# A hybrid mLSTM/HGRN2 layer on one core: first HGRN gates behind the last branch, and several steps moved in front of others on VectorE, ScalarE and SP

## The chip, the core and the metric

The kernel runs on one core of a Trainium2 chip. The metric is the device time of one execution in microseconds (us); lower is better. Before the change, three executions took 1135.51, 1135.64 and 1136.43 us; the median is 1135.64.

The core's engines run side by side, each through its own queue of instructions in order: TensorE (PE; its weight loads are listed as PEld), VectorE (DVE), ScalarE (ACT), GpSimd (POOL) and SyncE (SP, which here only issues transfers). They wait for each other through semaphores.

## The reference, cut to what matters

One layer over 512 prompt frames and 32 frames of a running stream (T = 544 columns, kept transposed: channels on partitions, frames along the free axis). All weights and data are float32.

```python
xn = _rmsnorm(h, norm_g[l])
proj = xn @ w_in[l]                       # 1024 -> 12296 columns
u, v_m, z_m, ig_pre, fg_pre, q_h, f_h, i_h, g_h, ga, gb = jnp.split(proj, ...)
c, conv_new = _causal_conv(u, ...); c = silu(c)
qm, km = per-head products of c; vm = v_m
hm, C_new, n_new, m_new = _mlstm(qm, km, vm, ig, lf, ...)     # 4 heads of 512
hm = (_head_layernorm(hm) + m_skip * c) * silu(z_m)
ya = hm @ w_brm
lfh = log(lb + (1 - lb) * sigmoid(f_h)); kh = (1 - lb) * sigmoid(-f_h); qh = silu(q_h)
oh, S_new = _hgrn(qh, kh, i_h, lfh, ...)                      # 8 heads of 128
oh = _head_rmsnorm(oh) * silu(g_h)
yb = oh @ w_brh
h = h + (sigmoid(ga) * ya + sigmoid(gb) * yb) @ w_out
h = h + sigmoid(h @ w_pg) * (p @ w_ple)
out = _rmsnorm(h, final_g)
```

## The kernel before, in words

**Matmuls.** Every float32 operand is split in a rounded high half and a remainder (`h` and `l` in the tile names): ScalarE casts the high half (L130), VectorE subtracts it (L131). A product takes three matmuls per 128x128 block: high weight by high data, high by low, low by high. The columns are handled in two halves of 272.

**Pairs of input units.** `w_in` is cut in units of 128 output columns. `Two` (L386) computes two units with a scheme of seven products of half size instead of eight. Each product is 12 matmuls of 128x272 with one weight piece; pieces made of plain weights are called `wa11`, `wa12` and `wa22` with the unit's number behind (wa126: form a11 or a12 of unit 6), those made of sums `ws1` to `ws4` (ws36: s3 of unit 6). `make` forms a piece (sums L448, split L130 and L131) some steps ahead, `run` issues its 12 matmuls into one of two PSUM banks (L485). After the products a11, s2 and s3, `keep` (L496) has ScalarE copy the bank to a tile `t` (L499), and later products add on into the same bank; `put` writes the results out (L506 to L510). A pair with `apart` makes its pieces at high priority.

**What sets the order.** TensorE runs in the order in which the program emits its matmuls (a manual schedule). `Pump` holds the remaining pieces as a list and emits them in between the steps of another stage: a stage is a generator that yields how many steps of the pump come before its next matmuls. The order on VectorE, ScalarE, GpSimd and SP is set by the framework's scheduler, from the program's order, priorities (`tc.high_priority()`) and explicit `tc.issue_after(...)`.

**Stages.** For each of the four mLSTM heads h: keys, queries, scores, then `mchain` (memory, layer norm) with the pieces of `fill(h)` between its steps. `fill(h)` holds the pairs of values, of z gates and the two u pairs of the next head. The tail of `mchain` transposes each of four 128-row tiles back into PSUM (`yt`, L1119 and L1120), adds the scaled transpose onto the skip term (L1125, L1126), multiplies by the z gate (L1127) and splits the result (`hm`, L103 and L104). Then `stage_br(h)` multiplies by `w_brm`: four weights `wbm` (two raw pieces each), two output tiles each, 24 matmuls per half of columns into banks `ya`. The partial sums over heads lie in DRAM: for h > 0 a tile `y` is loaded from `ya_d` (L1139), the banks are added (L1145), and it is stored again (L1146).

Behind mLSTM come eight HGRN heads. Their pairs of units are computed by a second pump, whose pairs (q0, f0) come ahead of `stage_br(3)`. When a pair is done, its `then` runs the gates: `forget` (ScalarE sigmoids L1410 to L1413) and `query` (sigmoids L1420 and L1421, VectorE products L1422 to L1425). `chain(h)` goes through seven levels (c = 1 to 64): ScalarE copies `km` (L1504), TensorE multiplies `pl` (L1515), VectorE updates the operands (L1539, L1542) and picks from the bank (L1546, L1550). It goes on with transposes `ht` (L1591), a state update `su` (L1610), the output `ho` (L1634), and at its end the head norm: squares on ScalarE, an rsqrt by 11 small VectorE instructions (L164 to L169), and the multiply by it (L1649, L1655). `finish(h)` transposes that output (`hoT`, L1663 and L1664) and gates it (L1667, L1668). It is emitted within the next head's chain, at level index 4. Where the ga gates are done, L1449 multiplies them onto the loaded `ya`.

Of the kernel before, what the change touches and what calls it, by code (L numbers as in the profile page):

```python
# [17 lines left out]
P = 128  # L18
# [46 lines left out]
def hybrid_step(ctx: ExitStack, tc: tile.TileContext, a, o):  # L65
# [321 lines left out]
    class Two:  # L387
# [4 lines left out]
        def __init__(self, outs, early=False, apart=False):  # L392
            self.keys, (self.unit, self.other), self.dests, self.thens = zip(*outs)
            self.sums, self.w, self.t, self.late, self.early, self.apart = {}, {}, {}, None, early, apart
            self.grows, self.alone = early or apart, False

        def begin(self):

# [33 lines left out]

        def make(self, *forms):
            def go(raw):
                with tc.high_priority() if self.apart else nullcontext():
                    for form in forms:
                        if form not in self.w:
                            self.form(form, raw)

            return go  # L440
# [55 lines left out]
        def keep(self, name, ps):  # L496
            t = tp.tile([P, TH], F32, tag="half", name=f"{name}{self.unit}", bufs=3)
            with tc.high_priority():
                S.copy(t, ps)  # L499
                self.t[name] = t  # L500

        def put(self, i, b, ps, t, how):
# [152 lines left out]
    def fill(h):  # L655


        def value(f, t):
            st8[h]["vt"][f] = t

        def gate(f, t):
            act = S.activation(t[:, :T], t[:, :T], AF.Silu)
            st8[h]["z"][f] = (t, act)

        def gate_one(f, acc):
            z = eslot(f"z{h}{f}")
            for b in range(2):
                with tc.high_priority():
                    out = V.tensor_copy(z[:, b * TH : (b + 1) * TH], acc[b][:, :TH])
            st8[h].setdefault("copies", []).append(out)  # L670
            act = S.activation(z[:, :T], z[:, :T], AF.Silu)
            st8[h]["z"][f] = (z, act)

        def inner_tile(f):
            ub = conv_tile((h + 1) * KH + f)
            return ub, conv_parts(ub)

        def inner(f, ub):
            st8[h + 1]["ub"][f] = ub
            if f == 0:  # L680
                conv(h + 1)

        st8[h]["z"] = [None] * KH
        todo = []
        if h:
            st8[h]["vt"] = [None] * KH
            todo += [pair("v", f, 16 + h * KH + f, lambda f: plain(eslot(f"vt{h}{f}")), value) for f in (0, 2)]
            todo += [pair("z", f, 32 + h * KH + f, lambda f: plain(eslot(f"z{h}{f}")), gate) for f in (0, 2)]
        else:
            todo += [One(("z", f), 32 + f, TH, lambda acc, f=f: gate_one(f, acc)) for f in range(KH)]  # L690
        if h + 1 < MH:
            st8[h + 1]["ub"] = [None] * KH
            todo += [pair("u", f, (h + 1) * KH + f, inner_tile, inner) for f in (0, 2)]
        return todo

    def stage_gates(fg, ig):
# [223 lines left out]
    def mchain(h, pump):  # L920
# [193 lines left out]
        for f in range(KH):  # L1114
# [7 lines left out]
            with tc.issue_after(act.ins):  # L1122
                S.mul(c[:, :T], c[:, :T], vcol(V_SK + ft))
            g = vcol(V_MG + ft)
            V.scalar_tensor_tensor(c[:, NS:T], pt[:, 0, :], g, c[:, NS:T], ALU.mult, ALU.add)  # L1125
            V.scalar_tensor_tensor(c[:, :NS], pt[:, 1, :NS], g, c[:, :NS], ALU.mult, ALU.add)  # L1126
            V.tensor_tensor(c[:, :T], c[:, :T], z[:, :T], ALU.mult)  # L1127
            hs.append(split(c[:, :T], f"hm{ft}"))
        t["hs"] = hs

    def stage_br(h):

        hs = st8[h]["hs"]
        for u in range(4):
            w = weight(a["w_brm"][h, u], f"wbm{h}{u}")
            for f in range(2):
                y = eslot(f"y{h}{u}{f}")[:, :T]
                if h:
                    nc.sync.dma_start(y, ya_d[u * 2 + f])  # L1139
                acc = dense(w, f * P, 256, P, hs, f"ya{h}{u}{f}")  # L1140
                for b in range(2):
                    if h == 0:
                        S.copy(y[:, half(b)], acc[b])
                    else:
                        V.tensor_tensor(y[:, half(b)], acc[b], y[:, half(b)], ALU.add)  # L1145
                nc.sync.dma_start(ya_d[u * 2 + f], y)  # L1146
            if h + 1 < MH and len(st8[h + 1]["cc"]) < KH:
                conv(h + 1)
# [247 lines left out]
    def units():  # L1396
# [19 lines left out]
        def query(h, qq):  # L1416
# [8 lines left out]
            V.tensor_tensor(kq[:, :T], q0[:, :T], kk[:, :T], ALU.mult)  # L1425
            hs[h].update(q0=q0, qq=qq)

        def value_tile(h):

            t = eslot(f"hi{h}")  # L1430
# [25 lines left out]
        for h in range(HH):  # L1456
            yield Two(
                [
                    (("q", h), 48 + h, lambda h=h: plain(both(h)[1]), lambda t, h=h: query(h, t)),
                    (("f", h), 56 + h, lambda h=h: plain((slot if h else eslot)(f"kq{h}")), lambda t, h=h: forget(h, t)),  # L1460
                ],
                h > 0,
                h == 0,
# [23 lines left out]
    def chain(h):  # L1487
# [10 lines left out]
        for li, c in enumerate(LEVELS):  # L1498
# [56 lines left out]
            if li == 0:  # L1555
# [5 lines left out]
                with tc.high_priority():  # L1561
                    V.tensor_reduce(
                        dg, pn.rearrange("p a t -> p (a t)")[:, : 5 * P].rearrange("p (b t) -> p b t", t=P), AX.X, ALU.add
                    )
            if li == 4 and h:
                yield 1
                finish(h - 1)

# [75 lines left out]
        for b in range(NB):  # L1644
            S.activation(osq, ov[:, b * P : (b + 1) * P], AF.Square, accum_out=hv[:, b : b + 1])  # L1645
        S.activation(osq, osb, AF.Square, accum_out=hv[:, NB : NB + 1])
        V.tensor_scalar(hv, hv, 1.0 / P, EPS, ALU.mult, ALU.add)
        rsqrt(hr, hv, P, 5)
        V.tensor_tensor(  # L1649
            ov[:, :NP].rearrange("p (b e) -> p b e", b=NB),  # L1650
            ov[:, :NP].rearrange("p (b e) -> p b e", b=NB),
# [17 lines left out]
        obf.append(ob)  # L1669
        hs[h].clear()  # L1670

    obf, held = [], []
    with tc.manual_schedule(engines={mybir.EngineType.PE}):
        pump = Pump(list(units()))

        pump.limit = pump.when["q", 0] // 2
        pump.to(pump.when["q", 0])
        stage_br(MH - 1)
        pump.limit = None
        for h in range(HH):  # L1680
            pump.to(pump.when["i", h])
# [208 lines left out]
```

## Time and profile before

| | |
|---|---|
| time of the profiled execution | 1136.49 us |
| its span | 1134.8 us |
| TensorE busy | 1118.7 us |
| VectorE busy | 901.9 us |
| ScalarE busy | 681.2 us |
| mean granted TensorE clock | 0.998 |

A row of a timeline gives the start in us, the duration, the engine, the line, the operation, what it writes and reads, its shape and how many instructions are put together; in brackets is the idle time of the engine before it and what ended that. A row of the list of waits gives the engine, its line and the line it waited for, the total in us, how often, and the longest. A row of a table of stretches gives the stretch, then the busy time of PE, PEld, DVE, ACT and POOL with the number of instructions, the granted TensorE clock, the share of the DMA engines that was busy, and GB/s.

A matmul of 128x272 is shown with about 0.29 us; in a steady row one starts every 0.125 us, since the duration covers the drain.

### The profile page before, as it was taken

How to read it: one execution, taken by the hardware profiler on the slowest of the kernel's cores; microseconds unless marked ns; L12 is line 12 of the kernel's file. 1: busy time of each engine (PE TensorE's matmuls, PEld its weight loads, DVE VectorE, ACT ScalarE, POOL GpSimd, SP SyncE). 2: the span in 40 equal slices, each digit the busy share in tenths (PEclk: the TensorE clock that was granted, in tenths of full speed). 3: DMA queues.
4: the chain of work that ended last, by engine and by line, in shares of the span. 5: the costliest groups of instructions: out<-in, count | busy, mean ns of one | idle time of the engine just before them, and what ended most of it. 6: DMA issues, size and time to landing. Idle time of an engine off the chain costs nothing.

```text
span 1134.8 us, 24055 instructions
## 1 busy us (share of the span) xinstructions
PE 1118.7 (99%) x8849; PEld 1103.6 (97%) x8849; DVE 901.9 (79%) x2034; ACT 681.2 (60%) x1537; POOL 180.0 (16%) x356
## 2 busy tenths in 40 slices
PE   9999999999999999999999999999999999999998
PEld 8999999999999999999999999999998999999998
DVE  6886998576896786976887699999999777654585
ACT  5677557655666555665665477777766567333462
POOL 4842010100011000101000123232232110000000
PEclk9999999999999999999999999999999999999999
DMA  6124224323444142552767665566666485332743
GB/s 236 57 96 130 82 75 152 124 90 108 135 152 151 49 131 104 160 166 70 232 169 224 183 150 140 139 138 136 156 147 163 123 219 162 115 103 70 264 146 116
DMA packets 89997, 157.85 MB, mean 139 GB/s; under 512 B 10132, under 2 KB 17684, under 8 KB 89880
## 3 DMA queue, kind: packets, MB, share of 16 engines
q1 hardware_dynamic: 80928, 140.27, 38.3%
q0 software_dynamic: 8784, 15.99, 9.1%
q8 instruction: 69, 1.13, 0.4%
q14 instruction: 48, 0.39, 0.1%
q10 hardware_dynamic: 168, 0.06, 0.0%
HBM read 131.37 MB, written 24.91 MB: 138 GB/s over the span
## 4 chain that ended last, share of the span: by engine, by line
PE 85%; DVE 9%; ACT 3%; issue 2%; DMA 1%; POOL 0%; SPq 0%; ACTq 0%; DVEq 0%
PE d L485 34%; PE ya L151 9%; PE pg L1740 4%; PE q L151 4%; PE yb L151 4%; PE o L151 4%; PE C L902 4%; PE k L151 4%; PE sc L862 3%; PE pl L1515 2%; PE nm L1077 2%; PE d L370 1%; DVE cv L634 1%; PE ple L151 1%; PE nm L1054 1%
## 5 line engine op out<-in xcount | busy, mean ns | idle before, releaser
L403 POOL DMA_DIRECT2D ws<-in_w_in x46 | 40.3, 876 | 231.7 <-DVE rsq_u L168 35.3
L499 ACT COPY t<-d 128x272 f32<-128x272 f32 x126 | 47.6, 378 | 5.1 <-PE d L485 5.1
L1539 DVE TENSOR_TENSOR hkq<-hkq,q 128x288 f32<-128x288 f32 (+1 forms) x96 | 40.7, 431 | 5.1 <-PE pl L1515 1.4
L634 DVE SCALAR_TENSOR_TENSOR cv<-ub,vec,cv 128x547 f32<-128x547 f32 x48 | 40.3, 841 | 1.3 <-ACT cv L629 0.6
L1515 PE MATMUL pl<-hkq,km 128*128 128x128 f32 x224 | 37.8, 291 | 0.9 <-ACT km L1504 0.7
L1504 ACT COPY km<-hkq 128x256 f32<-128x256 f32 x56 | 24.0, 429 | 16.9 <-DVE hkq L1539 8.1
L1515 PEld LDWEIGHTS pl<-hkq,km 128*128 128x128 f32 x224 | 31.2, 189 | 2.6 <-ACT km L1504 2.0
L1006 DVE SCALAR_TENSOR_TENSOR c<-c,wi,Cs 128x258 f32<-128x258 f32 x32 | 15.3, 477 | 20.0 <-PE Cs L1004 19.9
L914 ACT COPY Co<-C 128x258 f32<-128x258 f32 x32 | 10.4, 378 | 29.1 <-PE C L902 22.4
L1145 DVE TENSOR_TENSOR y<-ya,y 128x272 f32<-128x272 f32 x48 | 19.0, 434 | 10.7 <-PE ya L151 10.3
L1546 DVE COPY_PREDICATED at<-lmask,pl 128x256 f32<-128x256 uint8 (+1 forms) x56 | 25.2, 450 | 0.0
L1088 ACT COPY y<-nm 128x516 f32<-128x516 f32 x16 | 9.4, 590 | 21.6 <-PE nm L1077 21.5
L460 POOL DMA_DIRECT2D ws<-in_w_in x15 | 15.5, 1032 | 33.5 <-DVE ws272l L131 28.0
L1483 POOL TENSOR_SCALAR_AFFINE_SELECT aa<-at 128x128 f32<-128x128 f32 x32 | 19.4, 638 | 8.9 <-DVE at L1546 8.9
L799 POOL COPY vsm<-vt 128x96 f32<-128x96 f32 x16 | 5.4, 347 | 88.8 <-ACT vt L510 45.3
L1077 PE MATMUL nm<-vhl,sh 128*128 128x258 f32 x112 | 18.3, 286 | 0.0
L1036 DVE BATCH_NORM_STATS2 bs<-y 128x6 f32<-128x512 f32 (+1 forms) x20 | 13.7, 687 | 5.5 <-ACT y L1088 5.4
L1727 DVE TENSOR_TENSOR h<-o,h 128x272 f32<-128x272 f32 x16 | 6.3, 436 | 14.5 <-PE o L151 14.5
L876 ACT CAST sh<-dm 128x512 fp32r<-128x512 f32 (+3 forms) x16 | 7.3, 459 | 16.6 <-DVE dm L870 16.6
L1645 ACT ACTIVATE osq<-kq 128x128 f32<-128x128 f32 x32 | 9.8, 305 | 12.4 <-DVE kq L1640 12.1
L978 POOL CAST vhl<-one 128x4 fp32r<-128x4 f32 x8 | 1.9, 243 | 95.8 <-PE nm L1077 95.8
L1714 DVE TENSOR_TENSOR gb<-yb,gb 128x272 f32<-128x272 f32 x16 | 6.3, 436 | 13.0 <-PE yb L151 13.0
(4490 smaller groups left out, 5083.3 us busy)
## 6 DMA issues: line engine op xcount, KB each, us to landing
ws<-in_w_in POOLq DMA_DIRECT2D x61, 256.0 KB, 4.7
ws<-in_w_in SPq DMA_DIRECT2D x46, 256.0 KB, 3.5
ya_d<-y SPq DMA_DIRECT2D x32, 272.0 KB, 2.6
y<-ya_d SPq DMA_DIRECT2D x24, 272.0 KB, 3.7
c<-in_C SPq DMA_DIRECT2D x16, 258.0 KB, 4.0
out_Cp<-Co SPq DMA_DIRECT2D x16, 258.0 KB, 2.4
out_Cs<-c SPq DMA_DIRECT2D x16, 258.0 KB, 2.8
x<-in_xT SPq DMA_DIRECT2D x8, 272.5 KB, 4.7
```

The source lines that it names most:

```text
L151: PE.matmul(both[b][:m, :TH], part(w, off + k * step, m, x), xx[:, half(b)], start=(k == 0 and j == 0), stop=(k == n - 1 and j == 2),)
L403: G.dma_start(t, w_in[u][:, i * WP : (i + 1) * WP], accum_op=ALU.add)
L485: PE.matmul(ps, ww[:, c], xx, start=(start and k == 0 and j == 0), stop=end, skip_group_check=not start,)
L499: S.copy(t, ps)
L634: V.scalar_tensor_tensor(cv[:, :547], ub[:, j : j + 547], vcol(V_CW + 4 * ft + j), cv[:, :547], ALU.mult, ALU.add)
L862: PE.matmul(pn[:, 0, :n], ks[f][x][:, j * P : (j + 1) * P], qs[f][y][:, NS + j * P : T], start=(f == 0 and i == 0), stop=(f == KH - 1 and ...
L902: PE.matmul(pn[g][:, :VH], kw[b][x][:, f * P : (f + 1) * P], vv[b][y][:, g * VH : (g + 1) * VH], start=(b == 0 and j == 0), stop=(b == NB ...
L1077: PE.matmul(pn[:, g, :VH], st[j][x][:, (i - j) * P : (i - j + 1) * P], vv[j][y][:, g * VH : (g + 1) * VH], start=(j == 0 and q == 0), stop ...
L1515: PE.matmul(pn[:, 0, b * P : (b + 1) * P], km[:, b * P : (b + 1) * P], view(qq, b * P, ((2 * c, P // (2 * c)), (HB + c, 2), (1, c))), star ...
L1539: V.tensor_tensor(x, x, d, ALU.mult)
L1546: V.copy_predicated(at[:, :n], lmask[:, li, :n], pn[:, 0, :n])
L1740: PE.matmul(ps, part(w, k * P, P, x), xx[:, c], start=(k == 0 and j == 0), stop=(k == KD - 1 and j == 2))
```

## The change

It has six parts.

1. The last u pair of each `fill(h)`, h < 3, forms its pieces at high priority (`urgent`).
2. The reads of the `yt` bank in the tail (L1125, L1126; L1127, L1128 in the new numbering) are at high priority.
3. The evictions of the branch's banks (L1143, L1145; now L1148, L1150) are at high priority.
4. The first weight of `stage_br(3)` (wbm30) is made behind the (q0, f0) pair's last kept copy.
5. `query` and `forget` of HGRN head 0 are emitted behind `stage_br(3)` instead of where the pair ends.
6. In `chain(6)` the small instructions of the rsqrt are at high priority, and `finish(6)` is emitted in `chain(7)` at level index 6 instead of 4.

```diff
@@ class Two
-            self.grows, self.alone = early or apart, False
+            self.grows, self.alone, self.urgent, self.kept = early or apart, False, False, None
...
-                with tc.high_priority() if self.apart else nullcontext():
+                with tc.high_priority() if self.apart or self.urgent else nullcontext():
...
             with tc.high_priority():
-                S.copy(t, ps)
+                self.kept = S.copy(t, ps)
                 self.t[name] = t
@@ fill
             todo += [pair("u", f, (h + 1) * KH + f, inner_tile, inner) for f in (0, 2)]
+            todo[-1].urgent = True
@@ mchain, tail
-            V.scalar_tensor_tensor(c[:, NS:T], pt[:, 0, :], g, c[:, NS:T], ALU.mult, ALU.add)
-            V.scalar_tensor_tensor(c[:, :NS], pt[:, 1, :NS], g, c[:, :NS], ALU.mult, ALU.add)
+            with tc.high_priority():
+                V.scalar_tensor_tensor(c[:, NS:T], pt[:, 0, :], g, c[:, NS:T], ALU.mult, ALU.add)
+                V.scalar_tensor_tensor(c[:, :NS], pt[:, 1, :NS], g, c[:, :NS], ALU.mult, ALU.add)
@@ stage_br
-    def stage_br(h):
+    def stage_br(h, after=None):
...
-            w = weight(a["w_brm"][h, u], f"wbm{h}{u}")
+            with tc.issue_after(after.ins) if after is not None and u == 0 else nullcontext():
+                w = weight(a["w_brm"][h, u], f"wbm{h}{u}")
...
                     if h == 0:
-                        S.copy(y[:, half(b)], acc[b])
+                        with tc.high_priority():
+                            S.copy(y[:, half(b)], acc[b])
                     else:
-                        V.tensor_tensor(y[:, half(b)], acc[b], y[:, half(b)], ALU.add)
+                        with tc.high_priority():
+                            V.tensor_tensor(y[:, half(b)], acc[b], y[:, half(b)], ALU.add)
@@ HGRN units
+        def behind(h, then, t):
+
+            if h:
+                then(h, t)
+            else:
+                later.append(lambda: then(h, t))
...
-                    (("q", h), 48 + h, lambda h=h: plain(both(h)[1]), lambda t, h=h: query(h, t)),
-                    (("f", h), 56 + h, lambda h=h: plain((slot if h else eslot)(f"kq{h}")), lambda t, h=h: forget(h, t)),
+                    (("q", h), 48 + h, lambda h=h: plain(both(h)[1]), lambda t, h=h: behind(h, query, t)),
+                    (
+                        ("f", h),
...
+                        lambda t, h=h: behind(h, forget, t),
+                    ),
@@ chain
-            if li == 4 and h:
+            if li == (4 if h < HH - 1 else 6) and h:
                 yield 1
                 finish(h - 1)
...
-        V.tensor_scalar(hv, hv, 1.0 / P, EPS, ALU.mult, ALU.add)
-        rsqrt(hr, hv, P, 5)
+        with tc.high_priority() if h == HH - 2 else nullcontext():
+            V.tensor_scalar(hv, hv, 1.0 / P, EPS, ALU.mult, ALU.add)
+            rsqrt(hr, hv, P, 5)
@@ main
-    obf, held = [], []
+    obf, held, later = [], [], []
...
-        stage_br(MH - 1)
+        stage_br(MH - 1, pump.todo[0].kept)
+        for then in later:
+            then()
```

The change moves instructions at three places of which the prediction speaks. (Numbers behind a tile's name tell its buffers apart; lines are those of each version, so L1649 becomes L1667, L1539 becomes L1556, L1449 becomes L1461, L1145 becomes L1150.)

The first place is VectorE in chain(7), from the products of level c=16 on. Before:

```order
L1539 TENSOR_TENSOR hkq_11960<-hkq_11960,q_12310 128x2x8x16
L1550 COPY_PREDICATED at_12551<-lmask,pl_12761 32x32 x4
L169 SCALAR_TENSOR_TENSOR hr<-rsq_u,hr 128x5
L1449 TENSOR_TENSOR ya_12748<-ya_12748,ga_12435 128x544
L1649 TENSOR_TENSOR kq_11487<-kq_11487,hr 128x512
L1655 TENSOR_SCALAR osb<-osb,hr 128x128
L1449 TENSOR_TENSOR ya_12782<-ya_12782,ga_12434 128x544
L1667 SCALAR_TENSOR_TENSOR ob_12791<-hoT_12785,vec,hg_11722 128x512
```

and now:

```order
L1556 TENSOR_TENSOR hkq_11960<-hkq_11960,q_12310 128x2x8x16
L1567 COPY_PREDICATED at_12551<-lmask,pl_12761 32x32 x4
L1667 TENSOR_TENSOR kq_11487<-kq_11487,hr 128x512
L1673 TENSOR_SCALAR osb<-osb,hr 128x128
L1556 TENSOR_TENSOR hkq_11960<-hkq_11960,q_12310 128x2x4x32
L1563 COPY_PREDICATED at_12551<-lmask,pl_12807 128x256
L1556 TENSOR_TENSOR hkq_11960<-hkq_11960,q_12310 128x2x4x32
L1461 TENSOR_TENSOR ya_12748<-ya_12748,ga_12435 128x544
```

The multiply by the rsqrt comes one place earlier, and both ya products behind it. On TensorE, hoT stood directly behind the last ws480 matmul; now 12 matmuls of ws288, a pl pair, 12 of ws188, 6 of ws388, a pl pair and 6 more of ws388 come between.

The second place is VectorE and SP at branch 3. SP issued before:

```order
L402 DMA ws_9200<-in_w_in 128x512
L120 DMA wbm32r_8907<-in_w_brm 128x512
L120 DMA wbm32r_8909<-in_w_brm 128x512
L120 DMA wbm33r_8981<-in_w_brm 128x512
L1139 DMA y_8771<-ya_d 128x544
L1139 DMA y_8802<-ya_d 128x544
```

and now:

```order
L402 DMA ws_9200<-in_w_in 128x512
L1142 DMA y_8757<-ya_d 128x544
L1142 DMA y_8788<-ya_d 128x544
L1142 DMA y_8831<-ya_d 128x544
L1142 DMA y_8862<-ya_d 128x544
L120 DMA wbm32r_8893<-in_w_brm 128x512
L120 DMA wbm32r_8895<-in_w_brm 128x512
L1142 DMA y_8905<-ya_d 128x544
L1142 DMA y_8936<-ya_d 128x544
L1151 DMA ya_d<-y_8757 128x544
L120 DMA wbm33r_8967<-in_w_brm 128x512
```

The first loads of y come ahead of the weights wbm32, and both of wbm33 behind the first store of y. On VectorE the gates L1422 to L1425 stood ahead of the first eviction; now they (as L1427 to L1430) stand between the third and the fourth pair of evictions.

The third place is VectorE in the tail of head 0, where the pieces of units 6 and 7 are formed. Before:

```order
L1127 TENSOR_TENSOR c_905<-c_905,z_2187 128x544
L104 TENSOR_TENSOR hm1l<-c_881,hm1h 128x544
L1126 SCALAR_TENSOR_TENSOR c_968<-yt_2452,vec,c_968 128x32
L104 TENSOR_TENSOR hm2l<-c_905,hm2h 128x544
L506 TENSOR_TENSOR ub_2276<-d_2275,t_2332 128x272
L1127 TENSOR_TENSOR c_968<-c_968,z_2266 128x544
L506 TENSOR_TENSOR ub_2393<-d_2392,t_2425 128x32
L506 TENSOR_TENSOR ub_2393<-d_2392,t_2425 128x240
L131 TENSOR_TENSOR ws36l<-ws_2474,ws36h 128x512
```

and now:

```order
L1127 SCALAR_TENSOR_TENSOR c_807<-yt_2373,vec,c_807 128x512
L508 SCALAR_TENSOR_TENSOR ub_2279<-d_2275,t_2370 128x272
L1127 SCALAR_TENSOR_TENSOR c_881<-yt_2405,vec,c_881 128x512
L1128 SCALAR_TENSOR_TENSOR c_807<-yt_2373,vec,c_807 128x32
L1128 SCALAR_TENSOR_TENSOR c_881<-yt_2405,vec,c_881 128x32
L131 TENSOR_TENSOR ws36l<-ws_2474,ws36h 128x512
L1127 SCALAR_TENSOR_TENSOR c_905<-yt_2427,vec,c_905 128x512
L1128 SCALAR_TENSOR_TENSOR c_905<-yt_2427,vec,c_905 128x32
```

ws36l stood behind all four tiles' reads, their four multiplies and three splits; now it stands behind the reads of the first two tiles.

More of the change, by code (lines that the diff above doesn't have):

```diff
@@ L1458, in units @@
                 [
-                    (("q", h), 48 + h, lambda h=h: plain(both(h)[1]), lambda t, h=h: query(h, t)),
-                    (("f", h), 56 + h, lambda h=h: plain((slot if h else eslot)(f"kq{h}")), lambda t, h=h: forget(h, t)),
+                    (("q", h), 48 + h, lambda h=h: plain(both(h)[1]), lambda t, h=h: behind(h, query, t)),
+                    (
+                        ("f", h),
+                        56 + h,
+                        lambda h=h: plain((slot if h else eslot)(f"kq{h}")),
+                        lambda t, h=h: behind(h, forget, t),
+                    ),
                 ],
```

## The prediction

> **What bounds the kernel now.** First the page's line of busy times.
>
> ```profile
> PE 1118.7 (99%) x8849; PEld 1103.6 (97%) x8849; DVE 901.9 (79%) x2034; ACT 681.2 (60%) x1537; POOL 180.0 (16%) x356
> ```
>
> TensorE works in one written-out order for 1118.7 of 1134.8 us. The change removes no matmul, so it can only win TensorE's stalls: 16.1 us of idle time, and matmuls that run slowly after one. Next the list of TensorE's waits, of which these belong to places that the change touches:
>
> ```profile
> PE hoT L1663 <- DVE kq L1649: 3.1, 1, 3.1
> PE d L485 <- DVE ws36l L131: 1.0, 1, 1.0
> PE d L485 <- ACT t L499: 0.9, 1, 0.9
> PE ya L151 <- DVE y L1145: 0.9, 2, 0.5
> PE d L485 <- DVE ws214l L131: 0.2, 1, 0.2
> PE d L485 <- DVE ws210l L131: 0.2, 1, 0.2
> ```
>
> That is 6.3 us. Idle time understates a stall, because a matmul's duration covers the drain after its last column. I therefore count from start to start: what lies between two matmuls beyond the steady step. The step is 0.125 us: the rows at 317.00 and 602.84 below each follow their predecessors by that.
>
> **The change, part by part.**
>
> *The HGRN head's output transpose (hoT).* In the sixth HGRN chain it stands behind the last ws480 matmul and waits for L1649, which multiplies by the rsqrt result.
>
> ```profile
> 876.43 0.28 PE L485 MATMUL d<-xh,ws480l 128*128 128x272 f32 x1
> 879.79 0.41 PE L1663 MATMUL hoT<-anti,kq 128*128 128x128 f32 x2 [3.08 <-DVE kq L1649]
> 880.29 0.37 PE L485 MATMUL d<-xfh,ws288h 128*128 128x272 f32 x1
> 884.15 0.61 PE L1515 MATMUL pl<-hkq,km 128*128 128x128 f32 x4
> ```
> ```profile
> 876.00:880.00 4.00, 0.92 (x8) 0.73 (x7) 3.95 (x14) 1.55 (x3) 0.54 (x2) 1.00 0.83 245
> 880.00:885.00 5.00, 5.00 (x31) 5.00 (x30) 3.48 (x7) 0.90 (x2) 0.80 (x1) 0.66 0.45 98
> ```
> ```profile
> 878.33 0.72 DVE L1449 TENSOR_TENSOR ya<-ya,ga 128x544 f32<-128x544 f32 x1
> 878.96 0.69 DVE L1649 TENSOR_TENSOR kq<-kq,hr 128x512 f32<-128x512 f32 x1
> ```
>
> From 876.43 to 880.29 are 3.86 us. One step (0.125) and the transposes themselves (879.79 to 880.29, 0.50) belong there, so 3.24 us are lost. The second loss is the clock: the two stretches show it at 1.00 and then 0.66. The 18 matmuls from 880.29 to 884.15 take 3.86 us where 18 steps would be 2.25, so 1.61 more. Together 4.85.
>
> VectorE is full there, 3.95 of 4 us, so what TensorE waits for is a place in VectorE's queue; the priority alone moves L1649 ahead of L1449, 0.63 us (878.33 to 878.96). What counts is that TensorE now runs 12 ws288, 12 ws188 and 12 ws388 matmuls (36 x 0.125 = 4.5 us) and two pl groups before it comes to hoT, past 882. L1649 then starts by 878.33, in L1449's place, and with its 0.69 and some 0.2 for L1655 is done by 879.2. The slack is about 3 us.
>
> What is late next? The pl of the level c=32 comes to TensorE's head at 876.43 + 0.125 + 12 x 0.125 = 878.06, and its operand is copied by ScalarE here:
>
> ```profile
> 877.79 0.39 ACT L1504 COPY km<-hkq 128x256 f32<-128x256 f32 x1
> ```
>
> It ends at 878.18, so TensorE waits 0.15 to 0.25. The next level's products follow L1655 on VectorE (879.2 to 880.3), its km on ScalarE ends near 880.7, and TensorE wants it near 880.9: it fits, barely. For the first ht transposes and the state update behind them I reckon 0.1 more. I take 4.85 - 0.3 = **4.55**. Bounds: 4.85 if nothing is late; 0.6 if the wait turns up at km or pl with its clock loss, so that only L1649's earlier place is won.
>
> [...]
>
> *Last u pair of fill at high priority, and the PSUM reads of the tail.* In fill(0) VectorE does the tail's multiplies and splits before the low half ws36l.
>
> ```profile
> 170.64 0.29 PE L485 MATMUL d<-xfl,ws36h 128*128 128x272 f32 x1
> 171.89 0.39 PE L485 MATMUL d<-xfh,ws36l 128*128 128x272 f32 x1 [0.97 <-DVE ws36l L131]
> 172.12 0.29 PE L485 MATMUL d<-xfh,ws36h 128*128 128x272 f32 x1
> ```
> ```profile
> 171.16 0.68 DVE L131 TENSOR_TENSOR ws36l<-ws,ws36h 128x512 fp32r<-128x512 f32 x1
> ```
> ```profile
> 163.15 0.62 ACT L130 CAST ws36h<-ws 128x512 fp32r<-128x512 f32 x1 [1.66 <-PE d L485]
> ```
>
> 170.64 to 171.89 is 1.25, less a step 1.13; the matmul behind follows after 0.23 instead of 0.125: 1.23. Each restart below costs this 0.10 too. The high half was there at 163.77, and ws36l now stands behind two transposes' reads, at about 164.4 instead of 171.16: gone, with 6 us to spare. The multiplies and hm splits that it overtakes are wanted only by branch 0, behind the pair. A later piece of the same pair:
>
> ```profile
> 176.42 0.28 PE L485 MATMUL d<-xl,ws46h 128*128 128x272 f32 x1
> 176.85 0.40 PE L485 MATMUL d<-xh,ws46l 128*128 128x272 f32 x1
> ```
>
> 0.30 + 0.10 = 0.40, now ahead of hm1l. In fill(1), and alike in fill(2) (the waits list has both at 0.2):
>
> ```profile
> 317.00 0.28 PE L485 MATMUL d<-xfl,ws210h 128*128 128x272 f32 x1
> 317.50 0.40 PE L485 MATMUL d<-xfh,ws210l 128*128 128x272 f32 x1 [0.22 <-DVE ws210l L131]
> ```
>
> 0.375 + 0.10 = 0.48, twice. Sum of this part 1.23 + 0.40 + 0.96 = **2.59**. Lower bound: ws48l, the last piece, keeps its place in VectorE's order and could inherit up to 0.3 in each fill, so 1.7; the upper bound is the sum.
>
> *The pair's kept copy before branch 3's first weights.* TensorE waits for the copy t out of PSUM; ScalarE casts wbm310h first.
>
> ```profile
> 602.84 0.29 PE L485 MATMUL d<-xfh,ws348l 128*128 128x272 f32 x1
> 604.04 0.40 PE L485 MATMUL d<-xfh,wa2248h 128*128 128x272 f32 x1 [0.91 <-ACT t L499]
> ```
> ```profile
> 603.61 0.38 ACT L499 COPY t<-d 128x272 f32<-128x272 f32 x1
> ```
>
> ws348l's last matmul ends at 603.13. With nothing ahead of it the copy runs from about 603.15 to 603.53 instead of from 603.61 to 603.99: **0.46** won. The rest of the wait is the copy itself, since wa2248 adds on into the same bank. The cast it overtakes is wanted by branch 3's second unit after 613. Bounds 0 and 0.46.
>
> *Branch 3's evictions and the HGRN gates behind them.*
>
> ```profile
> 612.97 0.42 PE L151 MATMUL ya<-hm15h,wbm301l 128*128 128x272 f32 x2
> 613.93 0.39 PE L151 MATMUL ya<-hm12h,wbm310h 128*128 128x272 f32 x1 [0.55 <-DVE y L1145]
> 614.63 0.40 PE L151 MATMUL ya<-hm12h,wbm310h 128*128 128x272 f32 x1 [0.31 <-DVE y L1145]
> 614.86 0.42 PE L151 MATMUL ya<-hm12l,wbm310h 128*128 128x272 f32 x2
> ```
> ```profile
> 611.65 0.72 DVE L1425 TENSOR_TENSOR kq<-q,hkq 128x544 f32<-128x544 f32 x1
> 613.43 0.44 DVE L1145 TENSOR_TENSOR y<-ya,y 128x272 f32<-128x272 f32 x1 [1.06 <-PE ya L151]
> ```
> ```profile
> 599.33 0.33 SPq L402 DMA_DIRECT2D ws<-in_w_in  x1
> ```
> ```profile
> 607.99 2.32 SPq L1139 DMA_DIRECT2D y<-ya_d  x5
> ```
> ```profile
> y<-ya_d SPq DMA_DIRECT2D x8, 272.0 KB, 5.4
> ```
>
> The losses are 613.93 - 613.10 - 0.125 = 0.71, 0.70 - 0.125 = 0.57, and 0.10: 1.38. The first eviction names TensorE, but its sum was long done: the second sum of 24 matmuls ends at 612.97 + 2 x 0.125 = 613.22, so the first ended 24 steps earlier, at about 610.2. Two other things hold it: the gates L1422 to L1425, through at 612.37, and the old y, loaded from DRAM: issued at 607.99, 5.4 us to landing, hence 613.4. The change moves both. The gates go behind the third pair of evictions, and SP issues the y loads ahead of the wbm32r and wbm33r loads, right behind the ws load of 599.33; issued anywhere before 605 they are there in time. The eviction then runs at about 610.4 to 611.2, two microseconds before its bank is wanted at 613.22: **1.38** won. If only the gates moved, the load would still hold it and nothing would be won (lower bound 0, below that the second rival).
>
> *The rest at nothing.* Eviction priority in branches 0 to 2, where the waits list shows no ya wait; the unchanged work of L1125 to L1128; h=0's copies around 144, where sums of the weights and a BatchNorm read change places and nothing on TensorE waits. Uncovered, one of these costs one VectorE instruction, 0.3 to 0.7 us.
>
> Sum: 4.55 + 2.59 + 0.46 + 1.38 = **9.0 us**. The profiled execution took 1136.49, so 1127.5 by it. The median of the runs is 1135.64, 0.85 less, by which it is 1126.6. I take 1127.0.
>
> **Rivals.**
>
> *The hoT wait only moves.* For it: VectorE is full before 880, and three level products now stand on the path there. Against: after 880 it is busy only 3.48 of 5 us, and L1649 gets 3 us of slack. Then the gain is 2.59 + 0.46 + 1.38 + 0.6 = 5.0: 1131. If the wait shrinks and the clock stays up, 1129.
>
> *The gates inside branch 3 become a link.* wbm33r can now be issued only behind the first store of y, about 611.3. It lands some 4.3 us later:
>
> ```profile
> DMA to landing us min/median/max: 4.1/4.3/4.6
> ```
>
> ```profile
> 605.84 0.42 ACT L1411 ACTIVATE tf<-kq 128x256 f32<-128x256 f32 x1
> ```
>
> Behind its cast (615.6 + 0.6) come the gates' sigmoids on ScalarE and L1422 to L1425 on VectorE, and behind those the fourth pair of evictions. Before, the gates took 6.5 us from this first sigmoid to the end of L1425 at 612.37, with other work between; those of hkq, an estimated 1.4, now come ahead of the cast. So they end at about 616.2 + 5.1 = 621.3 at the latest, and the fourth bank is wanted at 613.22 - 0.46 + 3 x 3.04 = 621.9. The evictions just fit, with a slack of 0 to 0.4. A landing 1 to 2 us later costs about that, so 1128 to 1129.
>
> *Slower.* It is the same link at its worst: wbm330l's split stands before the third pair of evictions on VectorE, so a late wbm33r stops both. The branch banks are all in flight and TensorE stands; beyond 3 us it gets the slow clock too, 1.6 us as at 880. With 9.0 won elsewhere, it ends slower than before by 0.2% (2.3 us) only from a delay of about 10 us. For it speaks that SP works in order and the store waits there; against, that loads of this size landed within 5.4 us in this stretch. It gives about 1138.
>
> *The change doesn't do what it says.* The stalls at ws36l, ws210l and ws214l pass on to ws48l or to the next conversion, and branch 3 gains nothing because y's slot comes free late: 4.55 + 0.46 + about 0.5 = 5.5, 1130.5.
>
> **How the numbers follow.** The forecast's own range is 1126 to 1128.5, with 0.60. The hoT wait moved: 0.14. The gates as link: 0.10. Passing on: 0.08. Slower: 0.05; the small rest, 0.03, is a gain that I don't see. The lowest sensible time has all 9.3 us of the upper bounds and some of the smaller waits nearby: 1125. The high end takes in the first and the fourth rival and a little beyond: 1132. A difference within 0.2%, 2.3 us, can't be told from no change here. All cases but the slower one, and a sum of two rivals with small odds, lie below 1133.3: faster 0.89, same 0.06, slower 0.05.
>
> **What would show it.** The clock stays at 1.00 between 876 and 890, and no hoT wait is listed; a pl wait on km of about 0.2 may be new. The rows for ws36l, ws210l, ws214l and for ya on y are gone; t at L499 shrinks to about 0.45. VectorE's first branch-3 eviction starts near 610.5. I am wrong if TensorE's idle total falls by under 4 us, if a new wait over 0.5 us appears in 615 to 625 or 877 to 890, or if the half clock comes back anywhere.

## The result, and the profile after

The changed kernel took 1129.68 us in the median of four executions (1129.19 to 1131.11), the kernel before 1136.04 (1135.51 to 1137.72, four executions). The ratio is 0.9944, with a 95% interval from 0.9926 to 0.9961. Timed again beside the mended kernel below it was 0.9935 (0.9922 to 0.9947), 1129.11 against 1136.66. So it is faster by 0.4 to 0.8%, in the medians by 6.4 and 7.6 us, where 9 were summed up. The profiled execution took 1129.4 us; its span is 1127.7 us, 7.1 less than before.

First the list of TensorE's waits, after the change (total in us, how often, longest):

```profile
PE pl L1532 <- ACT km L1521: 1.2, 3, 0.7
PE Cs L1005 <- DVE c L1007: 1.0, 3, 0.5
PE d L485 <- ACT t L499: 0.8, 2, 0.5
PE yt L1120 <- DVE c L1128: 0.7, 1, 0.7
```

Of the six waits that the prediction listed, five are gone: hoT, ws36l, ws210l, ws214l and ya. The copy t at L499 is there twice now, 0.5 once as foreseen and 0.3 in a new place, and a wait of the yt transposes on a VectorE read of the tail is new. TensorE's idle time fell from 16.1 to 11.6 us, and its busy time from 1118.7 to 1116.1.

Around hoT the table of stretches answers to the rows shown before (PE, PEld, DVE, ACT and POOL busy, clock, DMA share, GB/s):

```profile
876.00:880.00 4.00, 4.00 (x34) 3.79 (x32) 3.97 (x11) 2.28 (x6) 1.18 (x2) 1.00 0.49 135
880.00:885.00 5.00, 4.97 (x42) 4.96 (x42) 4.94 (x10) 3.80 (x13) 1.97 (x4) 1.00 0.59 160
```

TensorE is busy through both, and the clock stays at 1.00 where 0.66 stood. VectorE is still full, but TensorE doesn't wait for it. From TensorE's and VectorE's timelines there:

```profile
875.34 0.69 DVE L1667 TENSOR_TENSOR kq<-kq,hr 128x512 f32<-128x512 f32 x1
```
```profile
878.12 0.61 PE L1532 MATMUL pl<-hkq,km 128*128 128x128 f32 x4
879.33 0.38 PE L1681 MATMUL hoT<-anti,kq 128*128 128x128 f32 x2
880.07 0.63 PE L1608 MATMUL ht<-ident,hi 128*128 128x128 f32 x4
```

The multiply is done at 876.03, hoT comes at 879.33: 3.3 us of slack.

Where the time went is best read by following one matmul through the executions. The table gives, for stretches between the first matmuls of two weight pieces, how much shorter (minus) the stretch was than in the profile before. (In the profile before, wi330 starts at 107 us, wbm000 at 178, wa1214 at 470, ws348 at 601, wa2248 at 604, wbm330 at 627, ws480 at 874, wa1182 at 888. "Again" is a second profile of the changed kernel.)

| stretch | predicted | after | again |
|---|---|---|---|
| head 0 with its tail, wi330 to wbm000 | -1.63 | -0.51 | -0.52 |
| heads 1 and 2, to wa1214 | -0.96 | -0.57 | -0.63 |
| to ws348 in head 3 | 0 | +0.13 | -0.03 |
| the kept copy, to wa2248 | -0.46 | -0.42 | -0.42 |
| branch 3, to wbm330 | -1.38 | -1.18 | -1.47 |
| seven HGRN chains, to ws480 | 0 | -0.32 | +1.89 |
| hoT and the clock, to wa1182 | -4.55 | -4.30 | -4.31 |
| before wi330 and behind wa1182 | 0 | +0.05 | -0.78 |
| sum | -8.98 | -7.12 | -6.27 |

Four rows came as forecast within 0.3 us. Head 0 won a third of its term, and the HGRN chains, which the change hardly touches, differ by 2.2 us between two executions of the same kernel.

### The profile page after: what moved, and what is told of

Its sections match the earlier page's. It is cut to its first block, busy times and chain, and to the rows that moved or that the text cites. A ratio compares the mean times of both kernels' runs of the same rounds, so it can differ in the third digit from the quotient of the medians.

```text
span 1127.7 us, 24054 instructions
## 1 busy us (share of the span) xinstructions
PE 1116.1 (99%) x8849; PEld 1101.9 (98%) x8849; DVE 899.9 (80%) x2034; ACT 682.4 (61%) x1537; POOL 189.0 (17%) x356
## 4 chain that ended last, share of the span: by engine, by line
PE 85%; DVE 8%; DMA 3%; ACT 2%; issue 1%; POOL 0%; SPq 0%; ACTq 0%; DVEq 0%
PE d L485 35%; PE ya L151 9%; PE pg L1760 4%; PE q L151 4%; PE yb L151 4%; PE o L151 4%; PE C L903 4%; PE k L151 4%; PE sc L863 3%; PE pl L1532 2%; PE nm L1078 2%; DMA ws<-in_w_in 2%; PE ple L151 1%; DVE cv L634 1%; PE ht L1608 1%
## 5 line engine op out<-in xcount | busy, mean ns | idle before, releaser
L499 ACT COPY t<-d 128x272 f32<-128x272 f32 x126 | 47.8, 379 | 10.3 <-PE d L485 10.3
L1556 DVE TENSOR_TENSOR hkq<-hkq,q 128x288 f32<-128x288 f32 (+1 forms) x96 | 40.8, 432 | 3.5 <-ACT t L499 1.0
L1150 DVE TENSOR_TENSOR y<-ya,y 128x272 f32<-128x272 f32 x48 | 18.8, 434 | 8.8 <-PE ya L151 8.8
L626 POOL COPY uo<-ub 128x3 f32<-128x3 f32 x16 | 18.0, 1125 | 33.9 <-DVE ub L508 27.4
```

Source lines behind the costliest of these rows:

```text
L499: self.kept = S.copy(t, ps)
L1556: V.tensor_tensor(x, x, d, ALU.mult)
```

## The experiments

**The changed kernel again, and a mended one.** In head 0's tail two stalls are new. TensorE, then ScalarE, then VectorE of the changed kernel:

```profile
156.37 0.39 PE L485 MATMUL d<-xfh,ws24h 128*128 128x272 f32 x1 [0.31 <-ACT t L499]
164.43 0.63 PE L1120 MATMUL yt<-ident,y 128*128 128x128 f32 x4 [0.66 <-DVE c L1128]
```
```profile
155.43 0.61 ACT L130 CAST wa116h<-wi6r 128x512 fp32r<-128x512 f32 x1
155.94 0.38 ACT L499 COPY t<-d 128x272 f32<-128x272 f32 x1
```
```profile
163.38 0.74 DVE L1127 SCALAR_TENSOR_TENSOR c<-yt,vec,c 128x512 f32<-128x512 f32 x1
164.04 0.40 DVE L1128 SCALAR_TENSOR_TENSOR c<-yt,vec,c 128x32 f32<-128x32 f32 x2
```

The urgent pair's first piece, wa116, is now cast ahead of the copy t, for which the ws24 matmuls wait. Before, the copy came first:

```profile
155.39 0.37 ACT L499 COPY t<-d 128x272 f32<-128x272 f32 x1
157.08 0.61 ACT L130 CAST wa116h<-wi6r 128x512 fp32r<-128x512 f32 x1
```

On VectorE, the long read of the second tile (163.38) stands before the short read of the first one (164.04), so the first bank is given back late, and the third transposes wait for it. The mended kernel changes those two things:

```diff
-                with tc.high_priority() if self.apart or self.urgent else nullcontext():
+                with tc.high_priority() if self.apart or (self.urgent and forms != ("a11",)) else nullcontext():
...
             with tc.high_priority():
-                V.scalar_tensor_tensor(c[:, NS:T], pt[:, 0, :], g, c[:, NS:T], ALU.mult, ALU.add)
                 V.scalar_tensor_tensor(c[:, :NS], pt[:, 1, :NS], g, c[:, :NS], ALU.mult, ALU.add)
+                V.scalar_tensor_tensor(c[:, NS:T], pt[:, 0, :], g, c[:, NS:T], ALU.mult, ALU.add)
```

> The changed kernel again, beside the mended one. First theory (the whole gain is the sum of TensorE's start-to-start losses, and two stalls that the change itself brings in at 156 and 164 us take 1.4 of it): 0.9935 to 0.9945 of before, 6.3 to 7.4 us less. Rival (the missing 2 us were a spread between executions): 0.992, 9 us less.

> The changed kernel with two edits: the first piece (form a11) of the urgent u pair keeps its ordinary priority, and of the two reads of a yt bank the short one (32 columns) comes first. First theory: the copy t at L499 is again ahead of wa116h on ScalarE, so ws24 starts without a wait (0.58 us); each bank is read to its end before the next one's, so the third yt transposes wait at most 0.1 us instead of 0.66; together 1.2 us less than the changed kernel, 0.9925 to 0.9935 of before. Rival (head 0 is not where it went; the HGRN chains take back what comes early because their weight sums still land when they did): both waits vanish and the end moves by under 0.4 us.

The changed kernel again: 0.9935 (0.9922 to 0.9947), as the first theory had it; 9 us are outside the interval. The mended kernel: 0.9933 (0.9919 to 0.9946). Both new waits are gone from its list, and head 0's stretch is 1.74 us shorter than before, where 1.63 was predicted and 0.5 measured without the mend. But the end doesn't show it: here the HGRN chains took 1.63 us longer than in the profile before. From TensorE's waits in the mended kernel:

```profile
PE pl L1532 <- ACT km L1521: 2.1, 4, 1.1
PE d L485 <- ACT t L499: 0.5, 1, 0.5
```

So the first theory is right on what the stalls cost and where, the two edits together; its 1.2 us for the whole was not to be seen behind a scatter of that size. The rival's "under 0.4 us" is what was measured at the end: 0.0002 in the ratios, and medians of 1129.11 us without and 1129.26 with the mend. Whether the chains take back what comes early, as the rival has it, is taken up under "The scatter".

**The two halves of the hoT part, one at a time.** On the kernel before, p6a has only the first edit, p6b only the second.

```diff
-            if li == 4 and h:
+            if li == (4 if h < HH - 1 else 6) and h:
```
```diff
-        V.tensor_scalar(hv, hv, 1.0 / P, EPS, ALU.mult, ALU.add)
-        rsqrt(hr, hv, P, 5)
+        with tc.high_priority() if h == HH - 2 else nullcontext():
+            V.tensor_scalar(hv, hv, 1.0 / P, EPS, ALU.mult, ALU.add)
+            rsqrt(hr, hv, P, 5)
```

> The kernel before, with finish(6) at level index 6 as the only change; the rsqrt keeps its low priority. First theory (what TensorE waited for was a place in VectorE's queue, and 36 matmuls of cover are enough without priority): no hoT wait, clock 1.00 from 876 to 890, wa1182 starts 4.0 to 4.8 us earlier than before, about 1131.5 us. Rival (the priority of the rsqrt is needed too): L1649 now stands behind the products of level c=32 on VectorE and hoT still waits 0.5 us or more; gain under 3.5 us.

> The kernel before, with the priority of the rsqrt as the only change; finish(6) stays at level index 4. First theory: L1649 moves ahead of one ya product only, so hoT still waits, 2.3 to 2.5 us instead of 3.1, and TensorE gains 0.6 us. Whether the half clock follows a wait of 2.4 us is open: if it does, wa1182 starts 0.6 us earlier; if the clock stays at 1.00, 2.2 us earlier. Rival (a late rsqrt was the cause): the wait falls below 0.5 us and the gain is over 4 us.

With the place alone the wait is gone, from TensorE's and VectorE's timelines of p6a:

```profile
881.44 0.38 PE L1663 MATMUL hoT<-anti,kq 128*128 128x128 f32 x2
882.34 0.63 PE L1591 MATMUL ht<-ident,hi 128*128 128x128 f32 x4 [0.20 <-DVE at L1546]
```
```profile
879.38 0.69 DVE L1649 TENSOR_TENSOR kq<-kq,hr 128x512 f32<-128x512 f32 x1
```

L1649 indeed falls behind the products of level c=32, but hoT still comes 1.4 us after its end, and ws480 to wa1182 is 4.14 us shorter: the place does it. Whether the priority adds anything isn't shown: with both edits the same stretch was 4.30 and 4.31 us shorter in the changed kernel, and 3.96 in the mended one. One execution of p6a took 1131.53 us, where the kernel before had a median of 1136.66 on the same chip. With the priority alone (1134.70 us) hoT waits 2.4 us, from p6b's TensorE timeline and stretches:

```profile
879.15 0.41 PE L1664 MATMUL hoT<-anti,kq 128*128 128x128 f32 x2 [2.37 <-DVE kq L1650]
```
```profile
880.00:885.00 5.00, 5.00 (x43) 5.00 (x42) 4.88 (x10) 2.19 (x5) 0.89 (x1) 1.00 0.52 119
```

0.71 us of the wait is won, and 1.56 more because the clock stays up: 2.27 in all. The second part stands on this one execution; the last section has how far the clock's part differed between others.

**Branch 3, one part at a time.** On the kernel before, p4 makes the first weight of branch 3 wait for the kept copy, p5 moves the gates of HGRN head 0 behind the branch. Neither changes the priority of the evictions.

```diff
 p4
-            w = weight(a["w_brm"][h, u], f"wbm{h}{u}")
+            with tc.issue_after(after.ins) if after is not None and u == 0 else nullcontext():
+                w = weight(a["w_brm"][h, u], f"wbm{h}{u}")
 p5
-                    (("q", h), 48 + h, lambda h=h: plain(both(h)[1]), lambda t, h=h: query(h, t)),
+                    (("q", h), 48 + h, lambda h=h: plain(both(h)[1]), lambda t, h=h: behind(h, query, t)),
```

> The kernel before, with only branch 3's first weight behind the pair's kept copy (the gates stay where they were). First theory (the parts on branch 3 need each other): wa2248 starts 0.45 us earlier, but wbm301 is now cast and split behind the gates' sigmoids and products, so TensorE stands in the first unit of the branch, 3 to 4.5 us in all; about 1139 us, and 1.6 us more if the clock halves. Rival (the parts add up): 0.4 us gained, nothing lost.

> The kernel before, with only the gates of HGRN head 0 behind branch 3 (no priority for the evictions, first weight unchanged). First theory: the loads of y come ahead of wbm32 by themselves, both things that held the first eviction are gone; wbm310 and wbm311 start 1.2 to 1.5 us earlier relative to wa2248, whose wait of 0.9 us stays. Rival (the priority of the evictions is what does it): under 0.5 us.

Alone, p4 makes the kernel slower: 1139.73 us in one execution, where the kernel before had a median of 1137.64 on the same chip. TensorE's waits and a stretch of p4:

```profile
PE ya L151 <- ACT wbm301h L130: 2.8, 1, 2.8
PE ya L151 <- DVE wbm301l L131: 1.2, 1, 1.2
```
```profile
612.00:616.00 4.00, 2.83 (x13) 2.77 (x13) 3.12 (x8) 0.93 (x3) 0.00 (x0) 0.62 0.43 136
```

0.42 us is won at the copy; then wbm301 stands behind the gates' sigmoids on ScalarE and their products on VectorE, 4.0 us of waits with the clock down to 0.62: wa2248 to wbm330 is 4.45 us longer. The two parts belong together.

With p5 (1136.47 us) the branch wins by itself; from VectorE's timeline:

```profile
610.86 0.79 DVE L1145 TENSOR_TENSOR y<-ya,y 128x272 f32<-128x272 f32 x2 [1.12 <-PE ya L151]
```

The eviction starts when its sum is there, wa2248 to wbm330 is 1.42 us shorter, and the wait for t is still 0.9. In this branch the eviction's priority is not needed.

**The scatter.** The kernel before was profiled once more.

> The kernel before once more, for its profile. First theory (the km waits in the HGRN chains scatter from execution to execution with the landing of the weight sums, and the profiled execution of before was a low one with 0.7 us): 0.5 to 2.5 us of pl waits on km here, in other places than before. Rival (they come with the change, which lets TensorE arrive earlier than the transfers): 0.7 us again, at the same two places.

Its pl waits were 0.5 us, at one place, so this run alone doesn't decide. Others help. p4, p5, p6a and p6b leave the chains before 870 as they are, and their pl waits on km over the whole execution were 0.9, 1.3, 1.1 and 1.1 us, their stretches from wbm330 to ws480 0.30, 0.77, 0.96 and 1.26 us longer than the first profile. In p1, below, the stretch was 0.19 longer. So the two profiles of before are the low end of a scatter of 1.5 us, without the change. With it the four stretches measured were -0.32, +1.89, +1.63 and, below, -0.46: a wider scatter. The averages differ little, 0.46 us in the seven profiles without the change and 0.69 in the four with it. That TensorE's early arrival lengthens the chains is not ruled out: of the six profiles that reach wbm330 first (by 625.92 us), five have chains 0.77 to 1.89 us longer than the first profile, but one (the first after the change) 0.32 shorter; the five others lie between -0.46 and +0.30. Whether the change adds to the scatter stays open.

The second profile of before also shows what held the first eviction of branch 3; from VectorE's timeline:

```profile
611.37 0.72 DVE L1425 TENSOR_TENSOR kq<-q,hkq 128x544 f32<-128x544 f32 x1
612.70 0.44 DVE L1145 TENSOR_TENSOR y<-ya,y 128x272 f32<-128x272 f32 x1 [0.61 <-DMA y<-ya_d]
```

The wait is now put down to the load of y, which landed 0.6 us after the gates were through; in p6a 0.16 us after. Branch 3 was 0.45 us and 0.92 us shorter in those two, without an edit there, and 0.42 and 1.05 in p6b and p1. So the 1.38 us of the first profile are the upper end. A part of what branch 3 "won" is probably a load that landed late in that one execution; its own profile doesn't name the load.

**An attempt on the chains.** In the mended kernel ScalarE's longest waits for transfers in the chains were these, and km stands behind such casts:

```profile
ACT ws475h L130 <- DMA ws<-in_w_in: 2.6, 1, 2.6
ACT ws455h L130 <- DMA ws<-in_w_in: 2.4, 1, 2.4
```

a_km4 puts every pair's last piece behind the current level's km:

```diff
             held.append(low)
+            pump.now = low
...
+                    if self.ids[self.made][1] == 6 and self.now is not None:
+                        after = self.now
```

> The mended kernel with one more edit: in the HGRN chains the casts and splits of every pair's last piece (form s4, whose weight sum is still being accumulated by a transfer) come behind the current level's copy km on ScalarE instead of behind the level's before it. First theory (between 630 and 860 us TensorE waits for km because km stands on ScalarE behind a ws4 cast that waits for its transfer, and this takes back 1 to 2 us of what is won before): the pl waits on km fall from 2.1 us to under 0.7, and the kernel ends 1 to 2 us below the mended one, 0.992 of before. Rival (the transfers bound the chains themselves): TensorE then waits for the ws4 pieces instead, as long as before; no change, 0.9933.

It took 1147.23 us, 1.0088 of before (1.0075 to 1.0102). Three of its waits, of TensorE:

```profile
PE d L485 <- DVE wa1155l L131: 1.8, 1, 1.8
PE d L485 <- DVE wa1151l L131: 1.8, 1, 1.8
PE pl L1535 <- ACT km L1523: 1.1, 6, 0.2
```

No km wait is longer than 0.2 us now, which fits the casts as the cause of the long ones. But the next pair's first pieces come behind them, and TensorE waits 1.8 us for each of six, 10.8 of the 17.1 us by which the chains are longer; the mean clock from 700 to 860 us was 0.96, by an estimate from that about 13 us at half clock. The first theory's gain is refuted, and the rival had the wrong piece and too small a price. No cure for the chains was found.

**Urgent pairs without the reads, and reads without priority.** p1 is the kernel before with only the urgent pair; a_urg_no2 is the changed kernel without the priority of the yt reads and with the first piece at ordinary priority.

```diff
 p1
-                with tc.high_priority() if self.apart else nullcontext():
+                with tc.high_priority() if self.apart or self.urgent else nullcontext():
...
+            todo[-1].urgent = True
 a_urg_no2 (against the changed kernel)
-            with tc.high_priority():
-                V.scalar_tensor_tensor(c[:, NS:T], pt[:, 0, :], g, c[:, NS:T], ALU.mult, ALU.add)
-                V.scalar_tensor_tensor(c[:, :NS], pt[:, 1, :NS], g, c[:, :NS], ALU.mult, ALU.add)
+            V.scalar_tensor_tensor(c[:, NS:T], pt[:, 0, :], g, c[:, NS:T], ALU.mult, ALU.add)
+            V.scalar_tensor_tensor(c[:, :NS], pt[:, 1, :NS], g, c[:, :NS], ALU.mult, ALU.add)
```

> The kernel before, with only the last u pair of each fill at high priority. First theory: this part alone wins the stalls at ws36l, ws46l, ws210l and ws214l (2.6 us) and brings in two smaller things: the copy t behind wa116h's cast (ws24 starts 0.4 to 0.6 us later), and ws48l, ws412l inherit 0.25 each; the third yt transposes do not wait. By branch 0's first weight it is 1.1 to 1.4 us ahead of where it was at ws24's predecessor, by HGRN's start 1.6 to 1.9. Rival (the priority of the yt reads is needed to bring ws36l forward): ws36l still waits 0.3 us or more.

> The changed kernel without the priority of the yt reads, and with the urgent pair's first piece at ordinary priority. First theory: the same as the mended kernel in head 0, no wait at ws24 and at the yt transposes, 1.6 to 1.9 us ahead of the kernel before at branch 0's first weight; the priority of the yt reads wins nothing anywhere. Rival (the reads at priority win something in heads 1 to 3): the gain from branch 0 to the end of head 3 is 0.3 us or more below the mended kernel's, which was 0.42 from wbm000 to ws348.

Here my theory fell. p1 took 1137.75 us beside 1136.78 for before, one execution each, so the stretches have to decide. ws36l, ws46l, ws210l and ws214l no longer wait, but from p1's list of waits:

```profile
PE yt L1120 <- DVE c L1127: 2.7, 5, 0.6
```

Five times a tail's transposes wait for a bank whose last read comes late, because urgent pieces stand before it. One of the five, on VectorE and then on TensorE:

```profile
310.09 0.69 DVE L131 TENSOR_TENSOR ws210l<-ws,ws210h 128x512 fp32r<-128x512 f32 x1
310.69 0.24 DVE L1127 SCALAR_TENSOR_TENSOR c<-yt,vec,c 128x32 f32<-128x32 f32 x1
```
```profile
311.09 0.63 PE L1120 MATMUL yt<-ident,y 128*128 128x128 f32 x4 [0.49 <-DVE c L1127]
```

From wi330 to wa1214, p1 is 1.42 us longer than before, not 1.6 to 1.9 shorter; without an edit there the second profile of before differs by 0.01. In a_urg_no2 (1130.83 us) the same line is

```profile
PE yt L1120 <- DVE c L1127: 3.9, 3, 1.7
```

and heads 1 and 2 take 2.52 us longer than before, where the mended kernel, which has the same first piece, won 0.70. So the rival was right: the reads' priority wins about 3 us in heads 1 and 2, as the other half of the urgent pair. (3.2 against the mended kernel, which also has the short read first, and 3.1 against the changed kernel, which also has the first piece urgent.)

## Why the prediction was right, and where a step failed

The forecast of 1127.0 had the sign and most of the size right; 1129.68 lies in the range of 1125 to 1132, but 1.2 us above the likeliest case's own.

- *hoT, 4.55.* Right: 4.30 and 4.31 measured, 3.96 in the mended kernel. The pl at level c=32 did come late, by 0.19 us from start to start (0.15 to 0.25 said), the ht transposes by 0.28 (0.1 said). That the place and not the rsqrt's priority counts was shown by p6a (4.14) and p6b (2.27). The bound of 0.6 for the priority alone kept the clock loss, which p6b didn't have.
- *The clock, 1.61 of it.* Right for the profiled execution, but not a constant. Five profiles have the same hoT wait, 3.08 us (3.1 in p1's list of waits): the first of before, r_before, p5, p1 and p4. p4's stretch behind it reads

```profile
885.00:890.00 5.00, 5.00 (x42) 5.00 (x42) 4.48 (x9) 2.00 (x5) 0.54 (x1) 1.00 0.60 123
```

with the clock at 1.00 also in the five microseconds before it, and ws480 to wa1182 is 1.54 us shorter for it. The number of matmuls at 0.227 us differed too: about 14, 8 and 10 in the first three, none in p4. The same idle time cost 0 to 1.6 us, so the forecast should have given the clock's part a range. Its "beyond 3 us it gets the slow clock" was an estimate from one wait in one execution; no run shows such a limit. In the timed executions the loss was there as a rule: all that are listed for the kernel before beside the variants have a mean clock of 0.998 or less, those of the changed kernel 0.999 or 1.0. (3.4 us at half clock take 0.0015 off the mean.)
- *Urgent pair and reads, 2.59.* This is the term that failed: 1.08 and 1.15 measured, below its lower bound of 1.7. The named stalls all went. The step that failed says that what ws36l overtakes "are wanted only by branch 0, behind the pair": it looked at the instructions that ws36l passes on VectorE, and not at those which wa116h passes on ScalarE (the copy t, 0.58 us) nor at the new order of the reads among themselves (the first bank's release, 0.66 us beyond a step). The mended kernel, without both, measured 1.74 in head 0 for the 1.63 predicted. In heads 1 and 2 the last piece inherited about 0.26 us each, which the lower bound had named; the row is ws48l:

```profile
318.01 0.28 PE L485 MATMUL d<-xl,ws48h 128*128 128x272 f32 x1
318.29 0.39 PE L485 MATMUL d<-xh,ws48l 128*128 128x272 f32 x1
318.52 0.28 PE L485 MATMUL d<-xh,ws48h 128*128 128x272 f32 x1
```

 The prediction also treated the two edits as one without saying that the first needs the second, and gave the reads no number of their own: p1 shows that the urgent pair alone is a loss, and beside it the reads' priority is worth about 3 us in heads 1 and 2.
- *The kept copy, 0.46.* Right: 0.42 in every version that has it. That it is worth anything only with the gates moved, p4 showed; the prediction costed it by itself.
- *Branch 3, 1.38.* Right in mechanism: both the gates and the late load held the eviction, and the load is named by the second profile. The size was that of one execution; in the four others without an edit there, branch 3 was 0.42 to 1.05 us shorter to begin with. With the first profile counted, the five average 0.57 us below it, the four that have the whole branch-3 part 1.32, so about 0.75 of the 1.38 is left.
- *The rivals.* The hoT wait did not move on. The gates as a link showed up at three tenths of a microsecond; the fourth pair of evictions ends at 621.08 and TensorE's matmul that takes over its bank is held:

```profile
620.30 0.78 DVE L1150 TENSOR_TENSOR y<-ya,y 128x272 f32<-128x272 f32 x2
```
```profile
620.82 0.71 PE L151 MATMUL ya<-hm12h,wbm320h 128*128 128x272 f32 x2
621.37 0.41 PE L151 MATMUL ya<-hm12l,wbm320h 128*128 128x272 f32 x2
```

 0.55 us from one start to the next where the rows around have 0.25; the slack of 0 to 0.4 was used up. "The change doesn't do what it says" came true for the small part of it, the passing on to ws48l.
- *Not in the forecast.* The HGRN chains as a source of 1 to 2 us of scatter. The sum was made against one profile, which lay low in the chains (the seven profiles without the change, itself counted, average 0.46 longer) and high in branch 3. An estimate of what is missing from the sum of 9.0, from the averages of the profiles: 1.5 in the urgent pair and reads, 0.3 at hoT, 0.6 in branch 3, 0.2 in the chains. That leaves 6.4, beside 6.4 and 7.6 in the medians.

## What to carry to other kernels

Raising the priority of one group of instructions is a change to everything that it passes, on each engine that it uses: list those per engine (here the copy t on ScalarE and the bank reads on VectorE) and ask who waits for each. Where two edits touch one queue, cost them singly and together; here two edits (the urgent pair, the early copy) were losses without their partners. And before a sum of stalls is made against one profile, see how long the stretches without any edit take in a second one.

## What the runs showed of the hardware that was not expected

The same wait of TensorE, 3.08 us to the hundredth, was followed by half clock for about 14, 8, 10 and 0 matmuls in four executions, and one of 2.37 us by none. In p4 a wait of 2.75 and one of 1.18 us, with 0.8 us of work between them, were followed by half clock too (0.62 over the four microseconds of the stretch shown), though each is shorter than the wait that p4's own hoT passed without it. In a_km4, where no wait in TensorE's list was longer than 1.8 us, the mean clock from 700 to 860 us was 0.96.

In the first profile of before, half clock stood from 880.69 to 884.10, 3.41 us. The stretch of that length ahead of it, and its own, are these:

```profile
877.27:880.69 3.41, 0.89 (x8) 0.92 (x9) 3.27 (x11) 0.90 (x2) 0.77 (x1) 1.00 0.83 285
880.69:884.10 3.41, 3.41 (x17) 3.41 (x17) 2.61 (x5) 0.90 (x2) 0.12 (x1) 0.50 0.51 86
```

TensorE idles for 2.52 us of the first. In p4 the same wait lies in the five microseconds

```profile
880.00:885.00 5.00, 1.92 (x17) 1.74 (x17) 4.88 (x14) 1.92 (x4) 0.81 (x2) 1.00 0.91 244
```

and the clock stays up, as it does in the next five, shown further up. Half clock lasted about as long in two other places. An estimate from the mean clocks of stretches gives 3.4 us at hoT in r_before (0.77 over 876 to 880, 0.84 over 880 to 885) and 3.4 us at branch 3 in p4 (0.62 over 612 to 616, 0.95 over 616 to 620). What differed at hoT is where it began: in the profile before 0.90 us behind the end of the wait at 879.79, with about 14 slow matmuls; in r_before, by the same estimate, at about 878.2, 0.6 us ahead of the end of the wait at 878.83, with 8.

So the length of a wait alone did not tell in these executions whether half clock followed, nor what it cost. What else decides was not shown; no run was made to test it. The clock that stayed up behind p4's hoT and in p6b is that of one execution each.
